# One weight stream through the mixing layers, later query/key transposes, a batched bias and layer-two values scaled in place

## The chip, the cores and the metric

The kernel runs on one core of a Trainium2 chip. The metric is the device time of one execution in microseconds (us). TensorE is called PE (its weight loads PEld), VectorE DVE, ScalarE ACT, GpSimd POOL, SyncE SP; SP issues most DMAs.

## The reference

A two-layer transformer on 256 image tokens (`x`) and 256 context tokens (`ctx`), width 1024, float32. Per layer:

```python
mod_l = split(silu(c) @ w_ada[l] + b_ada[l], 6);  mod_c = split(silu(c_ctx) @ w_ada[l] + b_ada[l], 6)
hy, fn, q, k, v, gate = split_in(modulate(x, g_mix[l], mod[0], mod[1]) @ w_in[l])   # 1024 -> 5632
q, k = rope(rms_norm(q)), rope(rms_norm(k))          # rope on image tokens only
mix = (sig(g1)*(hyena(hy) @ w_hy) + sig(g2)*(fourier(fn) @ w_fn) + sig(g3)*(diff_attention(q,k,v) @ w_at)) @ w_out
x = x + mod[2] * mix
n = modulate(x, g_ffn[l], mod[3], mod[4])
x = x + mod[5] * peer(n)      # scores against 2*128 keys, top 16 of 8 heads, 16384 gated rank-one experts
```

In layer two the context tokens give only keys and values, so most of its work is 256 tokens wide.

## The kernel before, in words

`mixing(l)` does everything up to `n`, `ffn(l)` the experts. The order is mixing(0), 0 to 570 us of the profile, ffn(0) to 1830, mixing(1) to 2140, ffn(1) to the end.

**Weights.** A weight chunk is 128x1024 float32. `wraw` (L138) loads it by a DMA from SP into one of 6 buffers `w4`, which the columns of `w_ada` share. `wsplit` (L143) makes a rounded high part `wh` (a cast on ACT, L106) and the remainder `wl` (a subtraction on DVE, L110), three buffers each. A float32 product is three matmuls, `wh`·`nh`, `wl`·`nh` and `wh`·`nl` (L98), where `nh`, `nl` are the same two parts of the activations. Mixing consumes 44 chunks of `w_in` in 22 groups, then 8 of `w_m` (the three branch matrices) and 8 of `w_out`; each consumer calls `wsplit(wraw(...))` where it needs the chunk.

**Mixing** goes in three phases. Phase 1: `proj_T` on groups 0 to 2 (hyena inputs, with a short convolution on DVE, L933 to L936). Phase 2: `proj_N` on groups 3 (Fourier input), 4 and 5 (queries), 6 and 7 (keys), 8 and 9 (values), with the steps of `hyena` driven in between. Phase 3: `proj_T` on groups 10 to 21 (gates), with `fnet` and `attention` driven in between. Then come `merge`, `out_proj` and the second normalization.

**Queries and keys.** For each group and each stream (s=0 image, s=1 context) `qk_norm` (L457) squares on ACT, reduces, takes a reciprocal root and scales on DVE (`qn`), for s=0 multiplies by the rope tables (`qr` on DVE, four small products `qt` on POOL, L479, and their sum on DVE, L482), then transposes four 128x128 blocks on PE (L487) and copies them to `qk` (L490, L492). Only attention in phase 3 reads `qk`.

**Modulation.** `ada(l, f)` computes column f of the modulation vectors `mods` for both streams: a product with a running sum on DVE (L171), then the bias on the one column (L175). With `side=True` (44 columns, during mixing(0)) the second stream goes another way: products on POOL (L167), sums on ACT (L168), and one DVE instruction that adds the two halves and the bias (L169). The other 40 columns, 4 at the start and 36 in the expert loops, use L171 and L175 for both streams.

**Second normalization.** `out_proj` gives x; `scaled` (L246) makes the normalized `xn` of each of 8 row blocks, on POOL or DVE (L248) and ACT (L250); `parted` (L253) splits them into `th`, `tl`; an ACT copy (L1034) puts them into `xf`, a part of the tile `acc`. In layer two the first matmuls of the router read `xf`.

**Order.** The kernel's lines give an order of the program, but a planner at compile time makes each engine's fixed instruction order from it: on each engine the earliest instruction of the program that its own estimate of times holds ready goes next. Its estimates are not the chip's times. Buffers are taken and freed in that plan as well; the small tiles of mixing, `qn`, `qr`, `pr` and others, share 24 slots `sl`.

Of the kernel before, what the change touches and what calls it, by code (L numbers as in the profile page):

```python
# [9 lines left out]
F32 = mybir.dt.float32  # L10
# [5 lines left out]
ALU = mybir.AluOpType  # L16
# [33 lines left out]
def tile_dit(ctx, tc, A, out, dbg=None):  # L50
# [71 lines left out]
    G.memset(epst, EPS)  # L122
    par = const.tile([P, 2, NPAR], F32, name="par")
    mods = const.tile([P, 2, 2, 48], F32, name="mods")
    ngain = const.tile([P, 2, 8], F32, name="ngain")
    rsl = const.tile([P, L], F32, name="rsl")
    sil = const.tile([P, 2, 1024], F32, name="sil")
# [15 lines left out]
    def wsplit(src, eng=None):  # L143
# [2 lines left out]
        split(hi, lo, src, eng)  # L146
        return hi, lo

    def drain(g):
        for _ in g:  # L150
            pass
# [4 lines left out]
    def ada(l, f0, f1, hold=False, side=False):  # L156
        for f in range(f0, f1):
            w = wraw(A["w_ada"][l, f])
            for s in range(2):
                m = mods[:, l, s, f:f + 1]  # L160
                b = pv(l, "b_ada")[:, f:f + 1]
                if side and s:
                    part = small([P, 2], name="part")
                    for h in range(2):
                        hs = slice(h * 512, (h + 1) * 512)
                        pr = slot(name="pr")
                        G.tensor_tensor(pr, w[:, hs], sil[:, s, hs], ALU.mult)  # L167
                        S.activation(pr, pr, AF.Copy, accum_out=part[:, h:h + 1])  # L168
                    V.scalar_tensor_tensor(m, part[:, 0:1], part[:, 1:2], b, op0=ALU.add, op1=ALU.add)  # L169
                    continue  # L170
                i = V.scalar_tensor_tensor(slot((P, 1024), BF16, "junk"), w, 1.0, sil[:, s],  # L171
                                           op0=ALU.mult, op1=ALU.mult, accum_out=m)
                if hold and s == 0:
                    pin(i)
                V.tensor_tensor(m, m, b, ALU.add)  # L175

    NSH = 4

# [161 lines left out]

    def proj_T(l, g, nh, nl, n, emit):
        for j in range(2):
            wh, wl = wsplit(wraw(A["w_in"][l, g, :, j * 1024:(j + 1) * 1024]))
            ps = pmt()
            for c in range(8):
                cs = slice(c * P, (c + 1) * P)
                mm3(ps[:, :n], wh[:, cs], wl[:, cs], nh[:, c, :n], nl[:, c, :n], c == 0, c == 7)
            emit(2 * g + j, ps)
            yield

    def proj_N(l, g, nh, nl, streams, emit):
        pss = {s: pmt((P, 2, L)) for s in streams}
        for j in range(2):
            wh, wl = wsplit(wraw(A["w_in"][l, g, :, j * 1024:(j + 1) * 1024]))
            for s in streams:
                for t in range(2):
                    ts = slice(s * L + t * P, s * L + (t + 1) * P)
                    for cc in range(4):
                        c = 4 * j + cc
                        cs = slice(cc * L, (cc + 1) * L)  # L360
                        o = pss[s][:, t]
                        mm(o, nh[:, c, ts], wh[:, cs], c == 0 and t == 0, False)
                        mm(o, nh[:, c, ts], wl[:, cs], False, False)
                        mm(o, nl[:, c, ts], wh[:, cs], False, c == 7)
                if j == 1:
                    emit(s, pss[s])
            yield
# [89 lines left out]
    def qk_norm(l, ps, s, w, hp, tabs, qk):  # L457
        f = ps.rearrange("p t c -> p (t c)")
        sq = slot(name="qs")
        S.activation(sq, f, AF.Square)  # L460
        ss = small([P, 8], name="ss")
        V.tensor_reduce(ss, sq.rearrange("p (g d) -> p g d", d=64), axis=AX.X, op=ALU.add)
        S.activation(ss, ss, AF.Sqrt, bias=epst, scale=1.0 / 64)
        V.reciprocal(ss, ss)
        xn = slot(name="qn")
        V.tensor_tensor(xn.rearrange("p (g d) -> p g d", d=64), f.rearrange("p (g d) -> p g d", d=64),
                        ss[:, :, None].to_broadcast([P, 8, 64]), ALU.mult)
        if s == 0:
            tb = tabs[w]
            xr = slot(name="qr")  # L470
            t2 = slot(name="qt")
            V.tensor_tensor(xr.rearrange("p (t h d) -> p t h d", t=2, h=2),
                            xn.rearrange("p (t h d) -> p t h d", t=2, h=2),
                            tb[:, :, None, 0:128].to_broadcast([P, 2, 2, 128]), ALU.mult)
            for t in range(2):
                v = xn[:, t * L:(t + 1) * L].rearrange("p (h g e d) -> p h g e d", h=2, e=2, d=16)
                o = t2[:, t * L:(t + 1) * L].rearrange("p (h g e d) -> p h g e d", h=2, e=2, d=16)
                for hf in range(2):
                    G.tensor_tensor(o[:, :, :, hf, :], v[:, :, :, 1 - hf, :],  # L479
                                    tb[:, t:t + 1, 128 + hf * 64:192 + hf * 64].rearrange(  # L480
                                        "p o (g d) -> p o g d", d=16).to_broadcast([P, 2, 4, 16]), ALU.mult)
            V.tensor_tensor(xr, xr, t2, ALU.add)  # L482
            xn = xr
        pt = pat((P, 2, L))
        for h in range(2):
            for t in range(2):
                T.transpose(pt[:, h, t * P:(t + 1) * P], xn[:, t * L + h * P:t * L + (h + 1) * P], ident)  # L487
        dst = qk[:, w, 2 * hp:2 * hp + 2, s * L:(s + 1) * L]
        if s == 0:
            S.copy(dst, pt)  # L490
        else:
            S.activation(dst, pt, AF.Copy, scale=pv(l, "g_q" if w == 0 else "g_k"))  # L492

    def lam_value(l, rows):
        li = 0.8 - 0.6 * math.exp(-0.3 * l)
# [62 lines left out]
    def merge(l, n, brh, brl, yh, yl):  # L558
        for g in range(4):
            for j in range(2):  # L560
                dt = 2 * g + j
                wh, wl = wsplit(wraw(A["w_m"][l, g, :, j * 1024:(j + 1) * 1024]))
                y = []
                for b, (c0, c1) in enumerate(((0, 2), (2, 4), (4, 8))):
                    ps = pmt()
                    for c in range(c0, c1):
                        cs = slice(c * P, (c + 1) * P)
                        mm3(ps[:, :n], wh[:, cs], wl[:, cs], brh[:, c, :n], brl[:, c, :n], c == c0, c == c1 - 1)
                    gt = slot(name="gt")
                    nc.sync.dma_start(gt[:, :n], gd[b * 8 + dt, :, :n])  # L570
                    S.activation(gt[:, :n], gt[:, :n], AF.Sigmoid)
                    V.tensor_tensor(gt[:, :n], ps[:, :n], gt[:, :n], ALU.mult)
                    y.append(gt)
                G.tensor_tensor(y[0][:, :n], y[0][:, :n], y[1][:, :n], ALU.add)
                G.tensor_tensor(y[0][:, :n], y[0][:, :n], y[2][:, :n], ALU.add)
                split(yh[:, dt, :n], yl[:, dt, :n], y[0][:, :n])

    def out_proj(l, n, yh, yl, x):
# [9 lines left out]
        late = 5 if n > L else 8  # L588
        held = []
        for dt in range(8):  # L590
            wh, wl = wsplit(wraw(A["w_out"][l, dt // 2, :, dt % 2 * 1024:(dt % 2 + 1) * 1024]))
            ps = pmt()
            if dt < late:
                part(dt, wh, wl, ps, 0, n)
                yield (dt,), 0, n, False
            else:
                held.append((dt, wh, wl, ps))
# [284 lines left out]

    def mixing(l, x, es):
        pools(es, f"m{l}", sl=24, sm=2)
        last = l == 1
        n = L if last else NT
        streams = (0,) if last else (0, 1)
# [56 lines left out]
        def emit_v(hp):  # L944
            def f(s, ps):
                S.copy(v[:, 2 * s:2 * s + 2, hp * L:(hp + 1) * L], ps)
            return f

        fs = iter([(0, f) for f in range(16, 40)] + [(1, f) for f in range(ADA_PRE)] if l == 0
# [19 lines left out]
        tabs = rope_tables(rows, rope, vx[:, 6:8])  # L969
        qk = b16t((P, 2, 4, NT), name="qk")  # L970

        def emit_qk(w, hp):
            def f(s, ps):
                qk_norm(l, ps, s, w, hp, tabs, qk)
            return f

        def phase2():
# [35 lines left out]
        nc.scalar.dma_start(x[:, :, :n], A["xT"] if l == 0 else xd[:, :, :n])  # L1013
        rs = slot(name="rs")
        gains(l, "g_ffn", 4)
        xns = [slot(name="xn") for _ in range(8)]
        tot = slot(name="tot")
        for cs, a, b, full in out_proj(l, n, yh, yl, x):
            for c in cs:
# [8 lines left out]
        for a in range(0, n, L):  # L1028
            for c in range(8):
                parted(c, xns[c], a, a + L, th, tl)  # L1030
        acc = b16t(name="acc")
        xf = acc.rearrange("p a b -> p (a b)")[:, 1024:1024 + 8 * min(n, NT - NG)].rearrange("p (c t) -> p c t", c=8)
        for c in range(8):
            S.copy(xf[:, c], xns[c][:, 0:xf.shape[2]])  # L1034
        if not last:
            for c in range(8):
                pt = pat((P, P))
                T.transpose(pt, xns[c][:, NT - NG:NT], ident)
                (S.copy if c % 2 else V.tensor_copy)(acc[:, c // 4, c % 4 * P:(c % 4 + 1) * P], pt)
# [207 lines left out]
```

## Time and profile before

| | |
|---|---|
| time, median of 3 runs | 2988.93 us (2986.04 to 2991.37) |
| profiled execution's own time | 2988.38 us |
| its span, first to last instruction | 2986.5 us |
| PE busy | 2852.1 us (96%) |
| DVE busy | 2225.1 us (75%) |
| ACT busy | 1263.9 us (42%) |
| POOL busy | 698.4 us (23%) |
| mean granted PE clock | 0.984 |

Busy time overlaps between engines. A busy PE isn't at its peak: a matmul counts as busy until its modelled end, and at a lower granted clock it takes longer. The time that PE stands idle is found by what released it afterwards.

### The profile page before, as it was taken

How to read it: one execution, taken by the hardware profiler on the slowest of the kernel's cores; microseconds unless marked ns; L12 is line 12 of the kernel's file. 1: busy time of each engine (PE TensorE's matmuls, PEld its weight loads, DVE VectorE, ACT ScalarE, POOL GpSimd, SP SyncE). 2: the span in 40 equal slices, each digit the busy share in tenths (PEclk: the TensorE clock that was granted, in tenths of full speed). 3: DMA queues.
4: the chain of work that ended last, by engine and by line, in shares of the span. 5: the costliest groups of instructions: out<-in, count | busy, mean ns of one | idle time of the engine just before them, and what ended most of it. 6: DMA issues, size and time to landing. Idle time of an engine off the chain costs nothing.

```text
span 2986.5 us, 43845 instructions
## 1 busy us (share of the span) xinstructions
PE 2852.1 (96%) x16000; PEld 2425.5 (81%) x16000; DVE 2225.1 (75%) x4457; ACT 1263.9 (42%) x2293; POOL 698.4 (23%) x594
## 2 busy tenths in 40 slices
PE   6979999999989999999999999899899999999999
PEld 2877678776668888888898897788788899889988
DVE  5966786797978888788888886746678657765665
ACT  2534564421443333333333334336423555555554
POOL 3445333430014334333443442300200000000000
PEclk8989999999999999999999999999999999999999
DMA  7424555233789889888989883235457977766662
GB/s 250 137 85 134 159 184 221 102 113 106 275 342 378 314 323 328 314 317 298 333 311 325 313 325 124 75 108 183 161 163 263 335 246 246 251 228 224 223 225 96
DMA packets 236648, 682.20 MB, mean 228 GB/s; under 512 B 23556, under 2 KB 94282, under 8 KB 233232
## 3 DMA queue, kind: packets, MB, share of 16 engines
q1 hardware_dynamic: 174192, 505.49, 49.0%
q0 software_dynamic: 38928, 140.35, 13.0%
q10 hardware_dynamic: 23312, 33.56, 3.1%
q8 instruction: 125, 2.05, 0.3%
q14 instruction: 91, 0.75, 0.1%
HBM read 612.20 MB, written 67.11 MB: 227 GB/s over the span
## 4 chain that ended last, share of the span: by engine, by line
PE 72%; DVE 13%; issue 5%; DMA 5%; POOL 3%; ACT 2%; SPq 0%; POOLq 0%; DVEq 0%; ACTq 0%
PE pm L98 45%; PE pa L98 26%; DVE og L747 3%; DMA a<-Hd 2%; DVE wl L110 1%; DVE oa L743 1%; DVE junk L171 1%; POOL pr L167 1%; DMA w<-in_w_ada_dram 1%; DMA Hd<-a 1%; DMA w<-in_u_dram 1%; POOL qt L479 1%; DVE junk L1093 1%; DVE ob L744 0%; DVE vl L110 0%
## 5 line engine op out<-in xcount | busy, mean ns | idle before, releaser
L110 DVE TENSOR_TENSOR wl<-w,wh 128x1024 fp32r<-128x1024 f32 x312 | 394.5, 1265 | 191.1 <-ACT wh L106 189.3
L106 ACT CAST wh<-w 128x1024 fp32r<-128x1024 f32 x328 | 343.3, 1048 | 453.5 <-PE pm L98 388.7
L98 PE MATMUL pm<-th,wh 128*128 128x256 f32 (+2 forms) x1680 | 531.8, 317 | 2.3 <-DVE th L254 2.3
L98 PE MATMUL pm<-tl,wh 128*128 128x256 f32 (+2 forms) x1680 | 529.6, 315 | 2.5 <-DVE tl L255 2.5
L98 PE MATMUL pm<-th,wl 128*128 128x256 f32 (+2 forms) x1680 | 529.1, 315 | 0.3 <-DVE wl L110 0.3
L110 DVE TENSOR_TENSOR vl<-wv,vh 128x512 fp32r<-128x512 f32 x512 | 346.4, 689 | 148.6 <-ACT vh L106 143.5
L106 ACT CAST vh<-wv 128x512 fp32r<-128x512 f32 x512 | 316.5, 622 | 298.1 <-PE pm L98 172.2
L98 PE MATMUL pa<-vl,ah 128*128 128x512 f32 x1024 | 402.1, 393 | 11.2 <-DVE vl L110 11.2
L98 PE MATMUL pa<-vh,ah 128*128 128x512 f32 x1024 | 400.1, 391 | 7.4 <-ACT vh L106 7.3
L98 PE MATMUL pa<-vh,al 128*128 128x512 f32 x1024 | 400.1, 391 | 1.1 <-DVE al L110 1.1
L98 PE MATMUL pm<-acc,w 128*128 128x256 f32 (+1 forms) x1280 | 355.7, 427 | 8.6 <-ACT acc L1034 8.6
L98 PEld LDWEIGHTS pm<-tl,wh 128*128 128x128 f32 x1680 | 320.2, 191 | 13.0 <-DVE tl L255 3.9
L98 PEld LDWEIGHTS pm<-th,wh 128*128 128x128 f32 x1680 | 320.4, 191 | 11.8 <-DVE th L254 2.9
L98 PEld LDWEIGHTS pm<-th,wl 128*128 128x128 f32 x1680 | 320.2, 191 | 5.1 <-DVE wl L110 0.6
L98 PEld LDWEIGHTS pm<-acc,w 128*128 128x128 f32 x1280 | 235.9, 191 | 78.0 <-ACT acc L1034 9.0
L106 ACT CAST ah<-a 128x384 fp32r<-128x384 f32 (+1 forms) x256 | 117.7, 460 | 295.2 <-DVE a L822 254.7
L98 PEld LDWEIGHTS pa<-vl,ah 128*128 128x128 f32 x1024 | 192.7, 188 | 53.9 <-DVE vl L110 16.6
L98 PEld LDWEIGHTS pa<-vh,ah 128*128 128x128 f32 x1024 | 193.0, 189 | 46.1 <-ACT vh L106 8.4
L98 PEld LDWEIGHTS pa<-vh,al 128*128 128x128 f32 x1024 | 192.6, 188 | 41.5 <-DVE al L110 1.6
L1075 POOL DMA_INDIRECT row<-in_ug_dram,ix x64 | 93.5, 1461 | 433.1 <-DVE junk L1093 237.0
L781 ACT ACTIVATE a<-pm 128x384 f32<-128x384 f32 (+1 forms) x256 | 110.9, 433 | 146.5 <-PE pm L98 144.9
L822 DVE TENSOR_TENSOR a<-a,gt 128x384 f32<-128x384 f32 (+1 forms) x256 | 122.8, 486 | 65.6 <-DMA a<-Hd 59.7
(313 smaller groups left out, 5450.6 us busy)
## 6 DMA issues: line engine op xcount, KB each, us to landing
w<-in_u_dram SPq DMA_DIRECT2D x256, 512.0 KB
wv<-in_v_dram SPq DMA_DIRECT2D x256, 512.0 KB
w<-in_w_ada_dram SPq DMA_DIRECT2D x92, 512.0 KB
w<-in_w_in_dram SPq DMA_DIRECT2D x88, 512.0 KB
Gd<-st SPq DMA_DIRECT2D x18, 2048.0 KB
gt<-Gd SPq DMA_DIRECT2D x64, 384.0 KB
w<-in_wq_dram SPq DMA_DIRECT2D x32, 512.0 KB
gt<-Gd SPq DMA_DIRECT2D x64, 256.0 KB
```

The lines of the kernel that those rows point to most:

```text
L98: T.matmul(o, l, r, start=start, stop=stop, skip_group_check=True)
L106: S.copy(hi, src)
L110: (eng or V).tensor_tensor(lo[:, ks], src[:, ks], hi[:, ks].bitcast(F32), ALU.subtract)
L167: G.tensor_tensor(pr, w[:, hs], sil[:, s, hs], ALU.mult)
L171: i = V.scalar_tensor_tensor(slot((P, 1024), BF16, "junk"), w, 1.0, sil[:, s], op0=ALU.mult, op1=ALU.mult, accum_out=m)
L479: G.tensor_tensor(o[:, :, :, hf, :], v[:, :, :, 1 - hf, :], tb[:, t:t + 1, 128 + hf * 64:192 + hf * 64].rearrange("p o (g d) -> p o g d", ...
L743: V.tensor_tensor(oa, row(0), iob, ALU.is_equal)
L747: V.tensor_tensor(og[:, w * HG:(w + 1) * HG], oa, gv[:, w * HG:(w + 1) * HG, None].to_broadcast([P, HG, P, 2]), ALU.mult)
L781: S.activation(a[:, :n], ps[:, :n], AF.Gelu)
L822: V.tensor_tensor(a3, a3, gts[b // GB][:, :, b % GB], ALU.mult)
L1075: nc.gpsimd.indirect_dma_start(out=r, out_offset=None, in_=src, in_offset=bass.IndirectOffsetOnAxis(ap=ix, axis=0))
L1093: pin(V.scalar_tensor_tensor(slot((P, 1024), BF16, "junk"), r, 1.0, ta, op0=ALU.mult, op1=ALU.mult, accum_out=hg[:, k:k + 1]))
```

## The change

- `stream(l)` makes one sequence of all 60 weight chunks of a mixing layer. Each call hands out a chunk already split and at once loads and splits the next, so in program order chunk k+1's load and split stand ahead of chunk k's matmuls and of what follows them.
- `qk_norm` returns a function that does the transposes and the copy. The caller keeps up to two such functions and runs the oldest when a third arrives; the last two run after the first value group's two copies.
- `ada` no longer adds the bias per column. After every eighth column one DVE instruction adds the halves (where the second stream went by POOL) and one adds the bias to 8 columns of both streams.
- In layer two `scaled` works directly in `xf`, so the copies at L1034 are gone there; in layer one each copy moves into the loop of the transposes (L1036).

```diff
     mods = const.tile([P, 2, 2, 48], F32, name="mods")
+    parts = const.tile([P, 2, 48, 2], F32, name="parts")
+    halved = set()
...
+    def stream(l):
+        def halves(name, gs):
+            for g in gs:
+                for j in range(2):
+                    yield A[name][l, g, :, j * 1024:(j + 1) * 1024]
+        src = chain(halves("w_in", range(22)), halves("w_m", range(4)), halves("w_out", range(4)))
+        ahead = []
+        def fetch():
+            s = next(src, None)
+            if s is not None:
+                ahead.append(wsplit(wraw(s)))
+        def get():
+            if not ahead:
+                fetch()
+            w = ahead.pop(0)
+            fetch()
+            return w
+        return get
...
                 m = mods[:, l, s, f:f + 1]
-                b = pv(l, "b_ada")[:, f:f + 1]
                 if side and s:
-                    part = small([P, 2], name="part")
+                    halved.add((l, f))
+                    part = parts[:, l, f]
...
-                    V.scalar_tensor_tensor(m, part[:, 0:1], part[:, 1:2], b, op0=ALU.add, op1=ALU.add)
                     continue
...
-                V.tensor_tensor(m, m, b, ALU.add)
+            if f % 8 == 7:
+                g = f - 7
+                while g <= f:
+                    e = g + 1
+                    while e <= f and ((l, e) in halved) == ((l, g) in halved):
+                        e += 1
+                    if (l, g) in halved:
+                        V.tensor_tensor(mods[:, l, 1, g:e], parts[:, l, g:e, 0], parts[:, l, g:e, 1], ALU.add)
+                    g = e
+                g = NSH if (l, f) == (0, 7) else f - 7
+                m = mods[:, l, :, g:f + 1]
+                V.tensor_tensor(m, m, pv(l, "b_ada")[:, None, g:f + 1].to_broadcast([P, 2, f + 1 - g]), ALU.add)
...
-            wh, wl = wsplit(wraw(A["w_in"][l, g, :, j * 1024:(j + 1) * 1024]))
+            wh, wl = scope["ws"]()            # the same in proj_N, merge and out_proj
...
-        pt = pat((P, 2, L))
-        for h in range(2):
...
+        def turn():
+            pt = pat((P, 2, L))
+            for h in range(2):
...
+        return turn
...
                 S.copy(v[:, 2 * s:2 * s + 2, hp * L:(hp + 1) * L], ps)
+                if turns:
+                    turns.pop(0)()
...
-                qk_norm(l, ps, s, w, hp, tabs, qk)
+                turns.append(qk_norm(l, ps, s, w, hp, tabs, qk))
+                if len(turns) > 2:
+                    turns.pop(0)()
...
-        xns = [slot(name="xn") for _ in range(8)]
+        acc = b16t(name="acc")
+        xf = acc.rearrange("p a b -> p (a b)")[:, 1024:1024 + 8 * min(n, NT - NG)].rearrange("p (c t) -> p c t", c=8)
+        xns = [xf[:, c] if last else slot(name="xn") for c in range(8)]
...
-        for c in range(8):
-            S.copy(xf[:, c], xns[c][:, 0:xf.shape[2]])
         if not last:
             for c in range(8):
+                S.copy(xf[:, c], xns[c][:, 0:xf.shape[2]])
```

## Rows read from the trace of the kernel before

**Rows 1.** The page, part 1: busy time of each engine.
```profile
PE 2852.1 (96%) x16000; PEld 2425.5 (81%) x16000; DVE 2225.1 (75%) x4457; ACT 1263.9 (42%) x2293; POOL 698.4 (23%) x594
```

**Rows 2.** Stretches by stage: length, then busy us (instructions), granted clock, DMA share, GB/s.
```profile
core 0: us, PE busy (x) PEld busy (x) DVE busy (x) ACT busy (x) POOL busy (x), PEclk, DMA share, GB/s
86.00:570.00 484.00, 445.41 (x2375) 367.29 (x2374) 359.52 (x634) 240.83 (x504) 212.95 (x167) 0.97 0.45 151
1830.00:2140.00 310.00, 270.85 (x1930) 242.19 (x1928) 205.15 (x380) 144.39 (x256) 66.28 (x90) 0.97 0.40 134
```

**Rows 3.** Waits of PE from 0 to 570: us in total, times, longest.
```profile
PE pa L487 <- DVE qr L482: 8.6, 3, 2.9
PE pa L487 <- DVE ss L464: 6.6, 1, 6.6
PE pa L538 <- DVE mods L169: 5.1, 4, 2.0
PE pa L538 <- DVE pp L534: 4.5, 7, 1.5
```

**Rows 4.** Waits of PE from 1800 to 2130.
```profile
PE pa L487 <- DVE qr L482: 5.8, 3, 2.4
PE pa L487 <- DVE ss L464: 0.8, 1, 0.8
```

**Rows 5.** PE in order of time around the fourth such wait of layer one.
```profile
226.09 0.86 PE L487 MATMUL pa<-ident,qr 128*128 128x128 f32 x4 [2.86 <-DVE qr L482]
...
228.03 0.41 PE L98 MATMUL pm<-wl,nh 128*128 128x256 f32 x1
228.24 0.41 PE L98 MATMUL pm<-wh,nl 128*128 128x256 f32 x1
...
230.00 0.28 PE L98 MATMUL pm<-wh,nl 128*128 128x256 f32 x1
230.12 0.28 PE L98 MATMUL pm<-wh,nh 128*128 128x256 f32 x1
```

**Rows 6.** Stretches around the four waits of layer one and one of layer two.
```profile
145.00:165.00 20.00, 13.40 (x74) 12.22 (x73) 14.35 (x20) 6.62 (x13) 11.76 (x10) 0.74 0.27 93
172.00:190.00 18.00, 15.09 (x95) 13.00 (x94) 13.31 (x21) 7.65 (x17) 9.56 (x8) 0.91 0.30 97
195.00:206.00 11.00, 8.14 (x42) 6.73 (x42) 7.27 (x11) 4.33 (x9) 5.01 (x6) 0.84 0.27 86
222.00:232.00 10.00, 7.14 (x44) 6.81 (x43) 8.29 (x9) 4.16 (x9) 9.98 (x9) 0.83 0.19 63
1908.00:1920.00 12.00, 9.60 (x69) 9.02 (x68) 7.41 (x14) 2.74 (x5) 3.56 (x5) 1.00 0.26 91
```

**Rows 7.** PE in order of time: a wait inside the hyena steps.
```profile
213.86 0.70 PE L98 MATMUL pa<-inv,ys 128*128 128x256 f32 x2 [2.95 <-POOL ys L404]
```

**Rows 8.** Groups of DVE from 0 to 570: busy us, mean ns, idle before.
```profile
L175 DVE TENSOR_TENSOR mods<-mods,par 128x1 f32<-128x1 f32 x52 | 31.3, 602 | 0.3
L169 DVE SCALAR_TENSOR_TENSOR mods<-part,par 128x1 f32<-128x1 f32 x44 | 19.0, 433 | 17.0 <-ACT pr L168 17.0
```

**Rows 9.** Line 175 alone: first 0 to 86, then its durations (min/median/max) from 900 to 1800.
```profile
0.00:86.00 86.00, 3.30 (x8) 0.84 0.65 226
...
L175 DVE TENSOR_TENSOR mods<-mods,par x54: 151/159/163, 907.5 to 1772.9; 128x1 f32<-128x1 f32 x54
```

**Rows 10.** DVE and POOL in order of time, 138 to 141.
```profile
139.51 1.12 DVE L175 TENSOR_TENSOR mods<-mods,par 128x1 f32<-128x1 f32 x1
...
138.35 2.27 POOL L167 TENSOR_TENSOR pr<-w,sil 128x512 f32<-128x512 f32 x1
```

**Rows 11.** ACT and PE in order of time at the end of mixing(1).
```profile
2135.05 3.79 ACT L250 ACTIVATE xn<-xn,mods,ngain 128x256 f32<-128x256 f32 x7 [2.86 <-POOL xn L248]
2139.11 0.60 ACT L250 ACTIVATE xn<-xn,mods,ngain 128x256 f32<-128x256 f32 x1 [0.27 <-POOL xn L248]
2139.62 2.53 ACT L1034 COPY acc<-xn 128x256 f32<-128x256 f32 x8
...
2140.06 1.22 PE L98 MATMUL pm<-acc,w 128*128 128x256 f32 x2 [8.62 <-ACT acc L1034]
```

**Rows 12.** Waits: the whole span, then SP from 80 to 460, then 86 to 570.
```profile
ACT wh L106 <- PE pm L98: 388.7, 179, 4.9
...
SPq L140 <- DVE junk L171: 137.2, 43, 7.8
...
POOL pr L167 <- DMA gd<-gr: 37.1, 7, 9.2
```

**Rows 13.** The chain of waits, a piece in phase 3: start, us, what.
```profile
325.06 4.10 DMA w<-in_w_in_dram
```

**Rows 14.** Waits of PE from 825 to 1800.
```profile
PE pa L98 <- DVE vl L110: 11.2, 10, 2.8
PE pa L98 <- ACT vh L106: 7.3, 1, 7.3
```

More of the change, by code (lines that the diff above doesn't have):

```diff
@@ L353, in proj_N @@
         for j in range(2):
-            wh, wl = wsplit(wraw(A["w_in"][l, g, :, j * 1024:(j + 1) * 1024]))
+            wh, wl = scope["ws"]()
             for s in streams:
@@ L483, in qk_norm @@
             xn = xr
-        pt = pat((P, 2, L))
-        for h in range(2):
[L486 to L492, printed above, removed]
+        def turn():
+            pt = pat((P, 2, L))
+            for h in range(2):
+                for t in range(2):
+                    T.transpose(pt[:, h, t * P:(t + 1) * P], xn[:, t * L + h * P:t * L + (h + 1) * P], ident)
+            dst = qk[:, w, 2 * hp:2 * hp + 2, s * L:(s + 1) * L]
+            if s == 0:
+                S.copy(dst, pt)
+            else:
+                S.activation(dst, pt, AF.Copy, scale=pv(l, "g_q" if w == 0 else "g_k"))
+        return turn
     def lam_value(l, rows):
@@ L561, in merge @@
                 dt = 2 * g + j
-                wh, wl = wsplit(wraw(A["w_m"][l, g, :, j * 1024:(j + 1) * 1024]))
+                wh, wl = scope["ws"]()
                 y = []
@@ L590, in out_proj @@
         for dt in range(8):
-            wh, wl = wsplit(wraw(A["w_out"][l, dt // 2, :, dt % 2 * 1024:(dt % 2 + 1) * 1024]))
+            wh, wl = scope["ws"]()
             ps = pmt()
@@ L884, in mixing @@
         pools(es, f"m{l}", sl=24, sm=2)
+        scope["ws"] = stream(l)
         last = l == 1
@@ L970, in mixing @@
         qk = b16t((P, 2, 4, NT), name="qk")
+        turns = []
         def emit_qk(w, hp):
             def f(s, ps):
-                qk_norm(l, ps, s, w, hp, tabs, qk)
+                turns.append(qk_norm(l, ps, s, w, hp, tabs, qk))
+                if len(turns) > 2:
+                    turns.pop(0)()
             return f
@@ L1030, in mixing @@
                 parted(c, xns[c], a, a + L, th, tl)
-        acc = b16t(name="acc")
-        xf = acc.rearrange("p a b -> p (a b)")[:, 1024:1024 + 8 * min(n, NT - NG)].rearrange("p (c t) -> p c t", c=8)
-        for c in range(8):
-            S.copy(xf[:, c], xns[c][:, 0:xf.shape[2]])
         if not last:
             for c in range(8):
+                S.copy(xf[:, c], xns[c][:, 0:xf.shape[2]])
                 pt = pat((P, P))
```

## The prediction

> **What bounds the kernel now.** I read the page's busy times first: PE is busy for 96% of the span, DVE for 75% [rows 1], so PE's idle and slow time is what can be won. The stretches by stage then show where that is: mixing of layer one leaves 484.0 - 445.4 = 38.6 us without PE work, mixing of layer two with the turn into the router 310.0 - 270.9 = 39.1 us [rows 2]. The edits touch these two stages, apart from the bias. Third, the waits of PE there say what ended each gap. The largest cause inside the loops is one line, the transposes of queries and keys (L487): 8.6 + 6.6 us in layer one [rows 3], 5.8 + 0.8 us in layer two [rows 4], eight gaps, one for each rotated group. The timeline shows the reason: the transposes stand in PE's order in the middle of the next group's matmuls, and PE holds them until L482 has added the POOL products, 2.86 us in the example [rows 5]. Everything behind them on PE waits too, though the next matmuls don't need them. Last, the timeline of the turn into the router shows PE released by the first copy into `xf` after 8.62 us [rows 11].
>
> What follows mixing needs its result and finds PE nearly full, so a microsecond won here should come through to the end.
>
> **The change part by part.** The sum is made against the profiled execution, 2988.38 us with a span of 2986.5 us; the median of the runs is 2988.93 us, 0.55 us more, and I add that at the end.
>
> *Transposes two steps later.* The gaps sum to 8.6 + 6.6 + 5.8 + 0.8 = 21.8 us [rows 3, 4]. After the change the transposes of a group stand behind the next group's matmuls in program order. A group of two streams is 96 matmuls; their pitch at full clock is 0.12 us [rows 5], so they come about 11.5 us later, against gaps of at most 6.6 us. What PE does instead is there already: the splits of the next chunks wait for a free buffer, that is for PE (388.7 us in 179 waits [rows 12]), not the other way round. Next late is hyena: its inverse transform waits 2.95 us for POOL [rows 7], and that chain, from the forward transform over DVE and POOL, does not get shorter when PE arrives sooner. I give a fifth of the 21.8 us to such waits and take 18 us. Bounds: 8 us, if hyena or the slots below keep most of layer one's share, and 22 us. Nothing else is added: the same transposes and copies run, and nobody needs `qk` before attention.
>
> *The clock behind the gaps.* After each of the four gaps in layer one the matmuls run at the lower level (1.2 of 2.4 GHz): pitch 0.21 us until it falls to 0.12 us [rows 5]. The mean granted clocks were 0.74, 0.91, 0.84 and 0.83 over 20, 18, 11 and 10 us [rows 6]; one minus the clock, times the length, is 5.2 + 1.6 + 1.8 + 1.7 = 10.3 us of full-speed work not done, of which part is idle time counted above: the first stretch has 6.6 us idle. Leaving that stretch at 1 to 3 us, the four cost 6 to 8 us. I take 6; bounds 2 (a shorter gap remains) and 8. In layer two the clock stayed at 1.00 [rows 6], so nothing there.
>
> *Bias by eight columns.* In mixing of layer one 52 + 44 small DVE instructions, 31.3 + 19.0 = 50.3 us [rows 8], give way to 11: six sums of biases (columns 4 to 7, 16 to 39 and the next layer's 0 to 15) and five sums of halves. The mean of 602 ns hides two kinds: where POOL only starts gathers the same instruction takes 159 ns [rows 9], beside POOL's products up to 1.12 us, and then it ends with POOL's instruction, 139.51 + 1.12 = 138.35 + 2.27 within 0.01 us [rows 10]. So a long one is mostly a wait for POOL.
>
> The Trainium skill, SBUF — State Buffer, section "Who interferes with whom", says that a DVE instruction with two SBUF inputs and a GpSimd one that reads SBUF share a port pair, and whichever comes second is blocked for the whole of the other. By that rule the next DVE instruction with two inputs inherits the block, so that only the short duration of each, 96 x 0.16 = 15 us of DVE time, would be freed instead of 50; the trace agrees on the block (rows 10), and no row shows the inheritance. By the rule the term below would be about a third of its upper end, 2 us, and the whole sum 30.5 us; without it 6 us and 34.5 us.
>
> DVE time counts only where PE waits on DVE: 5.1 + 4.5 us at attention's transposes [rows 3]. I take 3 of these 9.6 us; bounds 0 and 6. At the start, columns 4 to 7 cost 3.30 us in eight instructions [rows 9] on a DVE that PE waits for, but a second weight split (like the wl beside it) may be put there in their place: 1 us, bounds -1 and 2.5. In the expert loop 54 instructions of 159 ns are 8.6 us of DVE, but PE waits there only 11.2 us for vl and 7.3 us for vh, of 975 us [rows 14]: 0, bounds 0 and 3.
>
> *Stream.* In steady state the split is already ahead by as many chunks as there are buffers (the 388.7 us above), so a program order that asks for one chunk changes little. Every get also issues a load on SP: `w_in` k+1 now goes ahead of `ada` k's column, and in `merge` `w_m` k+1 ahead of the gates `gt` of k. The first helps where a late load stood on the chain, 4.10 us once [rows 13]; the second can delay a sigmoid. Splits also gain precedence over attention's DVE and ACT work, which may lengthen the gaps at L538. I take 0; bounds -8 (seven more gaps like the average 9.6/11 = 0.9 us there, and 2 us at merge) and +3.
>
> *Values in place.* ACT does all eight `scaled` first, the last ending at 2139.11 + 0.60 = 2139.71, then the copies, the first of which releases PE at 2140.06 [rows 11]. In place, PE can start behind the first `scaled`, at 2135.05 + 0.6, and only the eighth block waits for 2139.7. Seven of the first eight matmuls are then done before, and those of the second half if the planner puts them between. I take 3.5 us; bounds 2 us (only part of the first chain early) and 2140.06 - 2135.65 = 4.4 us. In layer one the copies only change places: 0, bounds -1 and 1.
>
> Sum: 18 + 6 + 3 + 1 + 0 + 3.5 = 31.5 us. 2988.38 - 31.5 = 2956.9; with the 0.55 us, and rounded up because the planner orders all of mixing anew and its estimates are wrong in places, 2958 us.
>
> **The rivals.**
>
> *Hyena takes the wait over.* PE arrives earlier, but the steps between hyena's forward and inverse transforms still pass DVE and POOL; POOL was busy 9.98 of 10 us in one stretch, DVE 8.29 [rows 6]. For it: the 2.95 us [rows 7]. Against: over layer one's mixing DVE has 484 - 360 = 124 us free and POOL more [rows 2], and hyena's result isn't needed before `merge`. If two thirds of the transposes' and the clock's 24 us come back in such waits: 2988.9 - 8 - 3 - 3.5 = 2974 us.
>
> *The transposes stay where they are.* The planner moves an instruction when its own estimate says that it is ready; where it believes PE idle, it can put the transposes early in spite of their place in the program. For it: the order in rows 5 is such an estimate gone wrong. Against: PE has matmuls to do at these places. Then only the rest is left, 2988.9 - 3.5 - 1 = 2984 us.
>
> *Slots run out: the slower side.* Two results are held for a group longer out of 24 slots, of which K, the hyena inputs, the Fourier inputs and the rows hold 5 + 6 + 2 + 1 = 14 throughout. POOL's products for `ada` already wait for slots (37.1 us for a slot that the gate store holds [rows 12]). If they wait longer, their column of `w_ada` keeps its w4 buffer, SP, which serves loads in order and already waits 137.2 us for such buffers [rows 12], issues `w_in` late, and PE runs out of weights. The price is the late load of 4.10 us [rows 13] for ten of the chunks of phase 2: 41 us against the 31.5, so 2988.9 + 9.5 = 2998 us. It decides from eight such late loads on (33 us). Against: no wait of PE on a weight load or split stands among the large ones, and the stream puts `w_in` ahead.
>
> **How the numbers follow.** Forecast 0.62, hyena 0.20, transposes unmoved 0.09, slots 0.09. The smallest difference that a measurement of this kernel tells from none is about 0.2%, 6 us; the fastest of three runs lies 5.3 us below the slowest. Of the third rival's 0.09 the half is within that, and of the slots rival's 0.09 some is too. Faster 0.83, same 0.09, slower 0.08. The lower bounds of all terms sum to 8 + 2 + 0 - 1 + 0 - 8 + 2 - 1 = 2 us, the upper ones to 22 + 8 + 6 + 2.5 + 3 + 3 + 4.4 + 1 = 50 us; the ends are unlikely together. The range 2942 to 2983 us takes in 47 us of gain, the forecast, the hyena rival and the edge of the third.
>
> **What would show it.** Right: waits of PE at the transposes of queries and keys under 3 us in all; the granted clock above 0.95 in the stretches around them; mixing of layer one shorter by some 24 us and layer two's by some 9; PE's gap before the router some 4 us instead of 8.6; 11 small instructions for 96 on DVE. Wrong: the waits on POOL's `ys` and `yc` or on `zn` grow by what the transposes lose; waits of PE on `wl` or on loads appear; or the transposes still stand inside the next group's matmuls. A gain in the expert loops would mean that DVE matters there, which I hold for nothing.

## The result and the profile after

The changed kernel takes 2956.83 us (median of 4 runs, 2953.78 to 2961.17) against 2990.15 for the kernel before in the same set of runs: 0.9894 of its time, 95% interval 0.9881 to 0.9906, so 28 to 36 us less (33.3 by the medians). The forecast was 2958 us. The profiled execution took 2953.98 us with a span of 2952.2, 34.3 us shorter than before.

Busy times of the engines after, as in [rows 1]:

```profile
PE 2844.7 (96%) x16000; PEld 2419.5 (82%) x16000; DVE 2198.4 (74%) x4306; ACT 1260.8 (43%) x2285; POOL 687.9 (23%) x594
```

PE is as full as before, and 7.4 us of its busy time are gone. 6.1 of them lie in phase 2, the stage with the transposes, where the same matmuls took 118.43 us at a mean granted clock of 0.93 before and take 112.36 us at 0.99 after. DVE has lost 26.7 us, far less than the instructions taken from it lasted; this is taken up below.

Stretches of the kernel after: the same four pieces of layer one as in [rows 6], then the two mixing stages, which answer to [rows 2]:

```profile
core 0: us, PE busy (x) PEld busy (x) DVE busy (x) ACT busy (x) POOL busy (x), PEclk, DMA share, GB/s
145.00:165.00 20.00, 20.00 (x145) 19.07 (x145) 16.37 (x22) 8.30 (x18) 11.89 (x12) 1.00 0.33 106
172.00:190.00 18.00, 18.00 (x119) 14.86 (x118) 15.76 (x23) 6.68 (x14) 9.19 (x10) 1.00 0.44 136
195.00:206.00 11.00, 11.00 (x78) 10.48 (x77) 6.08 (x8) 5.15 (x9) 4.01 (x7) 1.00 0.30 98
222.00:232.00 10.00, 10.00 (x79) 9.52 (x78) 5.09 (x3) 7.00 (x13) 8.89 (x6) 1.00 0.44 152
86.00:555.00 469.00, 447.14 (x2411) 366.61 (x2410) 346.95 (x628) 242.38 (x508) 217.50 (x174) 0.99 0.47 157
1807.00:2110.00 303.00, 273.42 (x1934) 244.94 (x1933) 203.37 (x378) 143.86 (x253) 67.10 (x90) 0.97 0.41 136
```

PE is busy throughout the four pieces, at a granted clock of 1.00 instead of 0.74 to 0.91. In layer one's mixing 469.0 - 447.1 = 21.9 us are left without PE work, from 38.6; in layer two's 29.6, from 39.1.

Waits of PE after, from 0 to 560 (the lines that answer to [rows 3], and hyena's: `zn` before its forward transform, `ys` and `yc` before its inverse one), then from 1770 to 2110 ([rows 4, 11]):

```profile
PE pa L577 <- DVE pp L573: 5.8, 8, 1.0
...
PE pa L98 <- POOL ys L439: 2.3, 1, 2.3
...
PE pa L98 <- ACT zn L416: 2.0, 1, 2.0
...
PE pa L577 <- DVE mods L206: 1.2, 1, 1.2
...
PE pa L98 <- POOL yc L438: 0.4, 1, 0.4
```

```profile
PE pm L98 <- ACT acc L285: 4.7, 1, 4.7
...
PE pa L98 <- POOL yc L438: 1.2, 1, 1.2
```

The transposes of queries and keys are in neither list: the 21.8 us are gone whole. Where [rows 5] showed a gap before such transposes, those of one image group now stand among matmuls that run at full pitch, 0.12 us apart:

```profile
176.81 0.28 PE L98 MATMUL pm<-wl,nh 128*128 128x256 f32 x1
176.93 0.28 PE L98 MATMUL pm<-wh,nl 128*128 128x256 f32 x1
177.05 0.60 PE L524 MATMUL pa<-ident,qr 128*128 128x128 f32 x4
177.41 0.36 PE L98 MATMUL pm<-wh,nh 128*128 128x256 f32 x1
```

The turn into the router, ACT and PE in order of time ([rows 11] before):

```profile
2104.98 3.79 ACT L285 ACTIVATE acc<-acc,mods,ngain 128x256 f32<-128x256 f32 x7 [2.86 <-POOL acc L283]
...
2106.12 9.66 PE L98 MATMUL pm<-acc,w 128*128 128x256 f32 x32 [4.75 <-ACT acc L285]
2109.04 0.60 ACT L285 ACTIVATE acc<-acc,mods,ngain 128x256 f32<-128x256 f32 x1 [0.27 <-POOL acc L283]
```

PE starts 1.14 us after the first `scaled` began, does 32 matmuls without a stop, and is over the wait after 4.75 us instead of 8.62.

Five marks on PE set the stages apart: hyena's first forward transform, the first matmul of `fnet`, the first matmul on `th`, the first matmul after ffn(0), the router's first. Before (the last is in [rows 11]), then after (the last stands above):

```profile
126.09 2.41 PE L98 MATMUL pa<-zn,fwd 128*128 128x512 f32 x5 [1.27 <-ACT zn L381]
262.70 1.54 PE L98 MATMUL pa<-fx,fd 128*128 128x256 f32 x6
536.23 0.39 PE L98 MATMUL pm<-th,wh 128*128 128x256 f32 x1 [0.81 <-DVE th L254]
1836.71 0.47 PE L98 MATMUL pm<-nh,wh 128*128 128x256 f32 x2 [4.39 <-DVE nh L254]
```

```profile
124.69 3.64 PE L98 MATMUL pa<-zn,fwd 128*128 128x512 f32 x4 [2.03 <-ACT zn L416]
239.77 1.97 PE L98 MATMUL pa<-fx,fd 128*128 128x256 f32 x8
511.14 0.39 PE L98 MATMUL pm<-th,wh 128*128 128x256 f32 x1 [0.80 <-DVE th L289]
1812.62 0.76 PE L98 MATMUL pm<-nh,wh 128*128 128x256 f32 x2 [4.39 <-DVE nh L289]
```

The stage between the first two, phase 2 with the transposes, went from 136.6 to 115.1 us and holds 21.5 of the 34.3 us. Phase 3 gave 2.2, ffn(0) lost 1.0, mixing of layer two with its turn went from 303.35 to 293.5 and gave 9.85; 1.4 us were there before the first mark, and ffn(1) gave 0.4. The same distances in single profiles of the experiments:

```
profile                      phase 2   phase 3   mixing two   span
before                        136.6     273.5      303.4      2986.5
later transposes alone        125.2     273.4      294.9      2965.3
bias alone                    132.5     272.3      302.8      2978.2
stream alone                  135.8     274.6      303.4      2989.3
values in place alone         138.7     273.2      300.5      2982.8
transposes and bias           116.8     273.7      295.3      2957.6
transposes and stream         125.1     274.7      298.1      2972.4
transposes and places         125.6     275.2      298.1      2972.9
all but the stream            116.8     273.6      296.4      2957.7
all but the stream, again     118.1     273.3      292.4      2959.0
after                         115.1     271.4      293.5      2952.2
after, again                  116.6     273.1      294.3      2954.6
after, one step later only    131.4     272.6      298.4      2975.1
```

Two profiles of one kernel differ by up to 1.5 us in phase 2, 1.8 in phase 3 and 3.9 in mixing two (the lines "again"), so a smaller difference between two lines tells nothing.

### The profile page after: what moved, and what is told of

Read it like the earlier page. It is cut to its first block, busy times and chain, and to the rows that moved or that the text cites. A ratio compares the mean times of both kernels' runs of the same rounds, so it can differ in the third digit from the quotient of the medians.

```text
span 2952.2 us, 43664 instructions
## 1 busy us (share of the span) xinstructions
PE 2844.7 (96%) x16000; PEld 2419.5 (82%) x16000; DVE 2198.4 (74%) x4306; ACT 1260.8 (43%) x2285; POOL 687.9 (23%) x594
## 5 line engine op out<-in xcount | busy, mean ns | idle before, releaser
L98 PE MATMUL pa<-vl,ah 128*128 128x512 f32 x1024 | 402.5, 393 | 11.5 <-DVE vl L110 11.5
```

The costliest lines, as they stand in the source:

```text
L98: T.matmul(o, l, r, start=start, stop=stop, skip_group_check=True)
```

## The experiments

Ratios are to the kernel before, run in turn with each kernel on one chip; microseconds are medians.

**Each edit alone.** The transposes first: `qk_norm` returns its last part as `turn()`, and the loop runs it two steps later.

```diff
...
+        turns = []
...
-                qk_norm(l, ps, s, w, hp, tabs, qk)
+                turns.append(qk_norm(l, ps, s, w, hp, tabs, qk))
+                if len(turns) > 2:
+                    turns.pop(0)()
```

> The kernel before with the later transposes alone. My theory: the waits of PE at the transposes of queries and keys (21.8 us) go, with them about 6 us of lower clock behind the four gaps of layer one, and a few microseconds come back as waits on hyena: 20 to 26 us faster, a ratio of 0.991 to 0.993. Rival, hyena takes the waits over: 6 to 12 us faster. Rival, the gain of the whole change comes mostly from the smaller DVE load: under 8 us.

Measured: 0.9944 (0.9931 to 0.9957), 2971.8 us, that is 16.8 us less (13 to 21). This is below my theory's 20 to 26 and above the rival's 6 to 12: the gaps at the transposes are gone, and part of it comes back. PE in the order of time shows where, a wait in hyena that the kernel before did not have and one on a weight split:

```profile
146.64 0.70 PE L98 MATMUL pa<-inv,yc 128*128 128x256 f32 x2 [3.65 <-POOL yc L403]
...
233.02 0.57 PE L98 MATMUL pm<-wl,nh 128*128 128x256 f32 x1 [2.69 <-DVE wl L110]
```

DVE of the same kernel ahead of the second wait:

```profile
223.55 1.23 DVE L175 TENSOR_TENSOR mods<-mods,par 128x1 f32<-128x1 f32 x1
224.70 1.33 DVE L169 SCALAR_TENSOR_TENSOR mods<-part,par 128x1 f32<-128x1 f32 x1
225.95 0.15 DVE L175 TENSOR_TENSOR mods<-mods,par 128x1 f32<-128x1 f32 x1
...
228.28 1.23 DVE L169 SCALAR_TENSOR_TENSOR mods<-part,par 128x1 f32<-128x1 f32 x1
...
231.75 1.22 DVE L110 TENSOR_TENSOR wl<-w,wh 128x1024 fp32r<-128x1024 f32 x1
```

The split that PE needs at 230.3 ends on DVE at 231.75 + 1.22 = 232.97. Its cast on ACT was done at 221.99; between lie products of `ada` of 2.3 us each and five bias instructions on single columns, three of them of 1.2 to 1.3 us, 3.7 us in all by their starts, and DVE has no idle time from 219 to 236 us. So DVE, which had been hidden behind PE's own gaps, is what is late next. The wait on `yc` has the same source by a longer way. DVE has next to no idle time from 112 to 138 us, so the `yt` of hyena's first half comes late; behind it wait POOL's product `yc` and the product for `ada` after it, behind that a sum and a cast on ACT, and behind the cast the split and the second half's `yt` on DVE. Hyena's first forward transform starts at 123.92 us here, so the first `yt` comes 10.33 us later; with the bias changed too (below) it starts at 126.61 us, and `yt` comes 7.77 us later. `yt` on DVE, with the transposes alone and with both:

```profile
134.25 0.68 DVE L400 TENSOR_TENSOR yt<-pa,K 128x512 f32<-128x512 f32 x1
...
134.38 0.68 DVE L412 TENSOR_TENSOR yt<-pa,K 128x512 f32<-128x512 f32 x1
```

The bias alone: halves are kept until eight columns are there, then one sum of halves and one of biases.

```diff
-                    V.scalar_tensor_tensor(m, part[:, 0:1], part[:, 1:2], b, ...)
...
-                V.tensor_tensor(m, m, b, ALU.add)
+            if f % 8 == 7:
...
+                m = mods[:, l, :, g:f + 1]
+                V.tensor_tensor(m, m, pv(l, "b_ada")[:, None, g:f + 1].to_broadcast(...), ALU.add)
```

> The kernel before with the bias by eight columns alone. My theory: 2 to 5 us faster, from shorter waits at attention's transposes and at the start. Of DVE's busy time: if the instruction behind a removed one inherits the wait for POOL, it falls by about 25 us (168 short instructions of 0.16 us less the 17 added); if the wait goes with the instruction, by about 55 us. Rival, DVE's load bounds mixing of layer one: 10 us faster or more.

Measured: 0.9982 (0.9974 to 0.9991), 2982.51 us, 6.1 us less by medians and 5.4 by the ratio. DVE's busy time fell from 2225.1 to 2198.1 us, 27.0. Groups of DVE over the whole span, of before:

```profile
L110 DVE TENSOR_TENSOR wl<-w,wh 128x1024 fp32r<-128x1024 f32 x312 | 394.5, 1265 | 191.1 <-ACT wh L106 189.3 <-issue 1.4
L171 DVE SCALAR_TENSOR_TENSOR junk<-w,sil 128x1024 bf16<-128x1024 f32 x124 | 160.3, 1294 | 0.0
L175 DVE TENSOR_TENSOR mods<-mods,par 128x1 f32<-128x1 f32 x124 | 42.6, 344 | 2.2
L169 DVE SCALAR_TENSOR_TENSOR mods<-part,par 128x1 f32<-128x1 f32 x44 | 19.0, 433 | 17.0 <-ACT pr L168 17.0
```

and with the bias alone changed:

```profile
L110 DVE TENSOR_TENSOR wl<-w,wh 128x1024 fp32r<-128x1024 f32 x312 | 399.8, 1282 | 204.3 <-ACT wh L106 203.5
L172 DVE SCALAR_TENSOR_TENSOR junk<-w,sil 128x1024 bf16<-128x1024 f32 x124 | 165.0, 1334 | 1.1
L187 DVE TENSOR_TENSOR mods<-mods,par 128x16 f32<-128x16 f32 (+1 forms) x11 | 4.0, 366 | 0.2
L183 DVE TENSOR_TENSOR mods<-parts 128x8 f32<-128x8 f32 (+1 forms) x6 | 3.1, 519 | 0.1
```

42.6 + 19.0 us went and 4.0 + 3.1 came, a difference of 54.5 us, of which half, 27.5 us, turned up again in instructions that were not touched: 5.3 us in the splits, 4.7 in the products with the running sum, the rest spread thinner. The blocks that the short instructions sat out are in part sat out by the next one. DVE's busy time is steady enough for this: 2222.8 to 2225.1 us in the six profiles with the bias by columns, 2195.8 to 2198.7 in the seven with the bias by eight. Of the time won, 4.1 us lie in phase 2. They are one gap: PE's longest wait at the transposes, 6.6 us in [rows 3], is 2.4 us in this kernel, while the other three stay at 8.6 us in all (PE's waits from 123 to 290):

```profile
PE pa L499 <- DVE ss L476: 2.4, 1, 2.4
```

The later transposes remove that whole gap, so this gain can't be had a second time beside them.

The stream alone: one generator of `w_in`, `w_m` and `w_out` halves, split one ahead.

```diff
-            wh, wl = wsplit(wraw(A["w_in"][l, g, :, j * 1024:(j + 1) * 1024]))
+            wh, wl = scope["ws"]()            # the same in proj_N, merge and out_proj
...
```

> The kernel before with the one stream of weights alone. My theory: within 3 us of before, since the splits already run ahead until they meet the three buffers. Rival one: loads of w_in come earlier and PE waits less in phase 3, 4 to 6 us faster. Rival two: splits displace attention's work on DVE and ACT, 4 to 8 us slower, with longer waits of PE at attention's transposes.

Measured: 1.0011 (1.0002 to 1.0019), 2991.61 us: 3.3 us slower, with an interval from 0.6 to 5.7. Its profile has the transposes' gaps as before, and no single wait accounts for the difference. The waits at attention's transposes, which the second rival expected longer, are 8.1 us in all for 9.6.

The values in place alone: in layer two `scaled` writes into `xf` itself.

```diff
-        xns = [slot(name="xn") for _ in range(8)]
+        xns = [xf[:, c] if last else slot(name="xn") for c in range(8)]
...
```

> The kernel before with the values of layer two scaled into place alone. My theory: 3 to 4.4 us faster, the gap of PE before the router of layer two falling from 8.6 to 4 to 5 us. Rival, PE's first matmuls only wait for the last scaled block instead: the gap starts earlier but the router's first scores come no earlier, under 1.5 us.

Measured: 0.9987 (0.9978 to 0.9995), 2984.55 us, 3.9 us less by the ratio. PE's gap in the order of time is as in the whole change, 4.76 us for 8.62:

```profile
2135.83 1.65 PE L98 MATMUL pm<-acc,w 128*128 128x256 f32 x3 [4.76 <-ACT acc L250]
```

The four alone sum to 16.7 + 5.4 - 3.3 + 3.9 = 22.7 us by their ratios; together they gave 31.7. By an estimate from the five intervals some 7 us of the difference could be noise, so nine microseconds are a hint that two edits need each other. The next runs ask which.

**How many steps.** The whole change, with the transposes one step later instead of two:

```diff
-                if len(turns) > 2:
+                if len(turns) > 1:
```

> The changed kernel with at most one transpose function kept instead of two, so each runs after the next stream's matmuls of the same half instead of after the next group's. My theory: what counts is that a whole group of 96 matmuls lies between; with one step the image stream's transposes are behind only 24 matmuls, 2.9 us, which the planner's estimate passes anyway, so most of the eight gaps of layer one and two come back: 10 to 22 us slower than the changed kernel, 2967 to 2979 us. Rival: any deferral is enough: within 3 us of the changed kernel.

Measured: 0.9957 (0.9943 to 0.997), 2974.86 us, 18 us slower than the whole change. The gaps are back, in PE's order of time:

```profile
150.98 1.01 PE L524 MATMUL pa<-ident,qr 128*128 128x128 f32 x4 [4.06 <-DVE ss L499]
171.61 1.09 PE L524 MATMUL pa<-ident,qr 128*128 128x128 f32 x4 [2.96 <-DVE qr L517]
192.98 1.09 PE L524 MATMUL pa<-ident,qr 128*128 128x128 f32 x4 [2.90 <-DVE qr L517]
```

A step is one stream of one group. The gaps in layer one are at the image stream's transposes, and for them the first step is only the context stream's last 24 matmuls, 2.9 us at 0.12 us each; two steps are 96 matmuls, 11.5 us. After one step `qr` is not there yet on the chip and PE stops as before; after two it is. Of the 21.8 us of gaps in both layers 16.7 us stay with one step.

**Pairs.** The transposes with the bias, and with the stream:

> The kernel before with the later transposes and the bias by eight, nothing else. Alone they gave 16.8 and 6.1 us by the medians, 22.9 us if they add. My theory: they give more together, because the wait on POOL's yc that the transposes alone left (3.65 us) hangs on a late DVE: the wait falls under 1 us, and the sum is 25 to 28 us, 2961 to 2964 us. Rival, plain addition: 2965 to 2968 us with the wait still there.

> The kernel before with the later transposes and the one stream, nothing else. My theory: the 2.68 us wait of PE on a weight split (wl) that the transposes alone brought goes, since the split now stands ahead; the 3.65 us on yc stays: 2968 to 2971 us. Rival, addition: the stream costs its 3 us here too and the wait on wl stays: 2974 to 2977 us.

Measured: with the bias 0.9905 (0.9892 to 0.9919), 2959.37 us, 28 us less, where 16.8 + 6.1 = 22.9 would be the mere sum (the intervals are 24 to 32, 13 to 21 and 3 to 8 us, so the times alone don't settle it); with the stream 0.9953 (0.9939 to 0.9967), 2974.2 us, about the sum of the two alone. My theory of the second pair was wrong: I had expected the stream to bring the split in time, and the wait is untouched (PE's waits from 100 to 290):

```profile
PE pa L98 <- POOL yc L426: 4.1, 2, 3.6
PE pm L98 <- DVE wl L110: 2.7, 1, 2.7
```

With the bias changed, DVE stands idle for 0.64 us until the cast of the same chunk is there, and the split ends at 225.97 + 1.59 = 227.56. Counted from hyena's first forward transform, which comes 2.7 us later in this profile, that is 8.1 us earlier. The row of DVE in that kernel:

```profile
225.97 1.59 DVE L110 TENSOR_TENSOR wl<-w,wh 128x1024 fp32r<-128x1024 f32 x1 [0.64 <-ACT wh L106]
```

PE's wait there is gone and the one on `yc` is 1.06 us, not under the 1 us that I had given but 2.6 less than 3.65, as much as the first `yt` is earlier (10.33 - 7.77). Together that is 5.3 us less of idle time. With it PE's busy time in phase 2 falls by 3.1 us, from 116.0 to 112.9, as the mean granted clock rises from 0.96 to 0.99. So the bias is worth 8.4 us of phase 2 beside the later transposes and 4.1 without them, and not through the same wait. The profiles agree: three with later transposes and the bias by columns (one of them in the next experiment) have the wait on `wl`, 2.7 us, and one on `yc` of 3.6 to 4.1; five with both edits have none on `wl` and at most 1.1 at a time on `yc`. Phase 2 takes 125.1 to 125.6 us in the three and 115.1 to 118.1 in the five, which is clear of the scatter.

**Buffers or instructions.** The new bias also gives each half its own place in `parts` instead of a rotating small tile. This kernel has the later transposes and the places, but still one bias instruction to a column:

```diff
-                    part = small([P, 2], name="part")
+                    part = parts[:, l, f]
```

> The later transposes alone, with the two halves of each POOL column kept in 96 places of their own instead of two buffers; the per-column bias stays on DVE. It asks why the bias by eight gives more beside the later transposes. My theory, the small DVE instructions make DVE late: nothing changes against the later transposes alone, 2968 to 2975 us, the wait on wl of 2.7 us and the wait on yc of 3.6 us stay. Rival, the two buffers held ACT and POOL back: the waits go and it comes to 2960 to 2965 us.

Measured: 0.9936 (0.9922 to 0.995), 2969.91 us, as with the transposes alone; both waits stay:

```profile
PE pa L98 <- POOL yc L404: 4.6, 2, 4.1
PE pm L98 <- DVE wl L110: 2.7, 1, 2.7
```

So it is the instructions on DVE that the transposes had made critical, not their buffers. The column instruction of the second stream also makes DVE stand idle for ACT's sum, 12.7 us in three stops in phase 2 with the transposes alone; how much this and how much the busy time counts was not separated.

**The whole without the stream,** and once more beside the whole change on one chip:

> The changed kernel without the one stream. My theory: a wait of PE on a split in phase 2, 2 to 3 us, comes back, so 1 to 3 us slower than the changed kernel, 2958 to 2960 us. Rival, the stream is a loss of 3 us wherever it stands: 2953 to 2955 us.

> The changed kernel without the one stream, once more, beside the changed kernel on the same chip. If the stream is a loss: 2 to 4 us faster than the changed kernel here too. If the stream is worth nothing either way: within 2 us of it. If it helps, as the shorter phase 2 of the profile says (115.1 against 116.8 us from the first zn matmul to the first fx matmul): 1 to 3 us slower.

> The changed kernel itself, once more, for the comparison without the stream: 2953 to 2960 us, a ratio of 0.988 to 0.991.

Measured: 0.988 (0.9864 to 0.9895), 2952.31 us; then 0.9884 (0.9869 to 0.9898), 2954.53 us, beside 0.9891 (0.9876 to 0.9905), 2956.15 us, for the whole. My theory, that leaving it out costs 1 to 3 us, did not come; the intervals overlap, and nothing can be told between the two kernels. No version beats the change by what can be measured.

## Why the prediction was right

**Transposes and clock.** I took 18 + 6 us, with a fifth of the gaps given back to hyena. In the whole change the gaps went completely and the clock was 1.00 in the four pieces. Phase 2 got 21.5 us shorter, 15.5 of idle and 6.1 of busy time, where its gaps and clock had 15.2 + 6, and hyena's waits stayed at 4.7 us in layer one (2.3, 2.0 and 0.4, from 3.0 and 1.3). So nothing came back there, and the fifth was too much. Alone the edit gave 16.8: the give-back that I put on hyena exists, with the late split as its other half, but only while the small bias instructions stand on DVE. In layer two the granted clock was at its upper level before ([rows 6]) and the term was the gap alone; its 6.6 us went, but single profiles of mixing two scatter too much to show that nothing else did.

**Bias.** This is the mis-sized term. I gave 3 us in attention and 1 at the start. Phase 3 shows 0.4 and 2.2 us in two profiles of the changed kernel, although the waits at attention's transposes fell from 9.6 to 7.0 as forecast; the main part of what it gives alone, 4.1 us, is in phase 2, for which I had nothing. Beside the later transposes the edit is worth 28.1 - 16.8 = 11.3 us (by an estimate from the two intervals some 6 us more or less). The step that failed is that I took DVE and the splits to be well ahead of PE in phase 2. I read that from 388.7 us in which casts wait for PE [rows 12], but that row is of the whole span. In phase 2 of the kernel before (126 to 263 us) the same wait is short:

```profile
ACT wh L106 <- PE pm L98: 16.1, 4, 4.9
```

With the transposes alone 3.7 us in one wait are left of it. My sum added terms against one profile, and one of them used up the slack that was there. The total came out by luck, as the two errors have opposite signs: I forecast 18 + 6 for the transposes and 4 for the bias, 28 us, and measured are 16.8 and, beside them, 11.3, 28.1 us.

The Trainium skill, SBUF — State Buffer, sections "Who interferes with whom" and "Summary: rules for kernel authors", has the engine that comes second blocked until the other engine's instruction has ended. What I drew from it, that the next two-input instruction on DVE inherits the block, is now borne out: half of the 54.5 us came back. By the rule only the short duration of each, 0.16 us for the 168 - 17 = 151 instructions that are fewer, would be freed, 24 us, and without it 54.5; measured are 27.0, so this case's trace agrees with what I drew from the rule. DVE's busy time was in any case the wrong measure of the edit's worth, since the place in the order counted, not the total.

**Start.** My 1 us can't be seen: the first matmul on `nh` came between 76.45 and 79.75 us in the profiles, and two kernels with the old bias had it at 76.99 and 76.87, so that the loads of the start scatter by more than the edit could give.

**Stream.** Nothing beside the other edits, as forecast. Alone it costs 3.3 us, within my bounds of -8 and 3 and just past the 3 us that I had given for that run; why is not settled, since no wait names it.

**Values in place.** 3.5 us forecast, 3.9 measured alone (1.5 to 6.6), with the gap at 4.75 us for my 4.

**The rivals.** Hyena's waits took over in part, in the kernel with the transposes alone. The transposes did not stay where they were; that rival's gaps are what one step leaves, 16.7 of 21.8 us. Slots did not run out: no wait on loads came into the loops.

Mixing of layer one ended 25.1 us earlier (forecast 24), layer two's was 9.85 us shorter (forecast 9, and within the scatter of single profiles); 11 small instructions took the place of 96 there, five sums of biases and six of halves where I had counted six and five.

## What to carry to other kernels

When a stall on the bounding engine is removed, look for the engine whose lateness it covered, and price the edits that relieve that engine after the removal, not against the old profile: the pair here was worth 28 us where the parts gave 16.8 and 6.1, and part of the 6.1 came from a gap that the other edit removes anyway. Slack read from a whole span says little of one stage. An operation that waits is moved past the point where its input is ready on the chip, not where a planner believes it; one step instead of two left 18 us on the table. A short instruction that the profile shows as long can be waiting for something that the next one will wait for instead, as half of the time was here.

## What was unexpected of the hardware

The same one-column instruction lasted 0.15 us or 1.2 to 1.3 us on DVE within the same piece of 12 us, and leaving DVE with 151 fewer of its 4457 instructions freed half of the time that they took. The few sums that remain spread as widely (durations in ns: shortest, median, longest):

```profile
L210 DVE TENSOR_TENSOR mods<-mods,par x11: 159/177/1254, 50.4 to 2540.8; 128x16 f32<-128x16 f32 x10, 128x8 f32<-128x8 f32 x1
...
L206 DVE TENSOR_TENSOR mods<-parts x6: 150/704/1252, 132.4 to 421.0; 128x8 f32<-128x8 f32 x5, 128x4 f32<-128x4 f32 x1
```

Behind gaps of 2.9 us before transposes the granted clock was lower in layer one ([rows 6], and 0.92 over 155 to 240 us with one step), while with the single wait on `yc` of 1.06 us it was 1.00 over 135 to 155 us in the kernel with transposes and bias.
